# High and low parts of the stationary operands stored in turn, at four distances modulo 256 bytes

## The chip, the cores and the metric

The kernel runs on one core of a Trainium2 chip. The metric is the device time of one execution in microseconds, and the median of the runs is compared. TensorE's granted clock was 0.999 over the profiled execution.

## The reference

A two-layer encoder trunk over 256 tokens of width 2048, all in float32. Layer 0 mixes tokens with a bidirectional mLSTM, layer 1 with a bidirectional HGRN2; each is followed by a gated MLP of inner width 5504 with a depthwise convolution of width 3:

```python
for layer in range(DEPTH):
    hn = rmsnorm(h, norm_mix_g[layer])
    if layer % N_MIXERS == 0:
        mix = mlstm_mixer(hn, mlstm_w_in[j], mlstm_b_gate[j], mlstm_head_g[j], mlstm_w_out[j])
    else:
        mix = hgrn_mixer(hn, hgrn_w_in[j], lower_bounds[layer], hgrn_head_g[j], hgrn_w_out[j])
    h = h + mix
    h = h + conv_glu(rmsnorm(h, norm_ffn_g[layer]), ffn_w_up[layer], ...)
return rmsnorm(h, final_g)
```

Nearly all of the arithmetic is in the projections: `hn @ w_in`, `y @ w_out`, `hn @ w_up` (2048 to 2 x 5504) and `... @ w_down`. The weights, some 440 MB, are read once.

## The kernel before

Every projection is done in split precision. A float32 value is written as a high part (rounded to the format `float32r`) and a low part (the rest, in the same format), and the product is made of three terms: high with high, high with low, low with high.

The work is a list of chunks (class `Chunk`). Chunks of kind "fm" give 256 output features with the tokens along the columns: the weights are the stationary operand of the matmul and the activations the moving one. For each of 16 k-blocks and each of two feature blocks there is a pair of matmuls: line 201, high weights with the 512 columns of `x` (256 tokens high, 256 tokens low), and line 208, low weights with the 256 high columns. The up projections (86 chunks in all), mLSTM's q and k and HGRN's q and gates (`w_bq`) are of this kind. Chunks of kind "tm" give 512 output features with the tokens along the partitions: the activations are stationary and the weights move. For each k-block and each half of the tokens there are three matmuls of 512 columns, lines 191 to 193. v, o and the gates of the mixers are of this kind with the normalised tiles `xt0` to `xt15` as stationary operand; the output projections and the down projections (function `project`) use the tiles `ya`, `yb` and `g`, kept under the tags `yt0` to `yt21` by `slot` (the first 16 in the pool `keep`, the others in the pool `ff`, whose first tile `lead` only moves the following ones). The last seven k-blocks of the last chunk run one token half after the other (lines 178 to 180).

The generator `split_weights` fetches 1 MB of weights at a time on SP's queue into `raw` (three buffers) and cuts it into pieces of 1024 columns. For each piece ScalarE writes the high part `wh` (line 146) and VectorE the low part `wl` as the difference (line 147). There are four buffers of each, and `stream` keeps `LOOK = 3` pieces made ahead. A piece lasts for four k-blocks of an "fm" chunk or two of a "tm" chunk. The first chunk cuts smaller pieces of 640 columns. The activations are split the same way by `split` (lines 213 and 214) and, in the MLP, at lines 832 and 833.

The other work (heads of the mixers, norms, convolution) is pushed as generators on a list `side` and advanced by a planned time (`side.tick`) between the matmuls. In HGRN's `head`, each of seven levels h = 1, 2, 4 ... 64 multiplies alternating blocks of h elements by a gate (lines 698 and 699, through the views `blocks` and `gview`, lines 630 to 636): at h = 1 single elements from two places in turn, at h = 2 two neighbours together.

In memory `wh`, `wl`, `x` and `yt` lie each as contiguous runs: 1024 columns of `wh` in one tile, 1024 of `wl` in another; in `x` and `yt` 256 high columns and then 256 low ones. The stationary operand of one matmul is 128 neighbouring floats. The sizes of the tiles are such that `xt`, `yt` (all 22), `wh` and `wl` all begin at the same place modulo 256 bytes.

Of the kernel before, what the change touches and what calls it, by code (L numbers as in the profile page):

```python
# [8 lines left out]
F32 = mybir.dt.float32  # L9
F32R = mybir.dt.float32r  # L10
I32 = mybir.dt.int32
AF = mybir.ActivationFunctionType
ALU = mybir.AluOpType
PSUM = bass.MemoryType.PSUM

P = 128
T = 256
D = 2048
KT = D // P
# [24 lines left out]
WB = 4  # L44
MIX = 5
LEAD = 48
FIRST = (0, 1, 2, 4, 7, 10, 13, 16)

HALF = 64
# [5 lines left out]
def trunk_kernel(ctx, tc, xT, x_d, fg_d, pp_d, cst_d, w_first, w_aq, w_ak, w_av, w_ao, w_aout,  # L55
                 w_bq, w_bv, w_bg, w_bout, w_up, w_down, out, mscr):
    nc = tc.nc
    act, dve, pool, pe = nc.scalar, nc.vector, nc.gpsimd, nc.tensor

    keep = ctx.enter_context(tc.tile_pool(name="keep", bufs=1))  # L60
    wpool = ctx.enter_context(tc.tile_pool(name="wpool", bufs=1))
# [8 lines left out]
    hmx = keep.tile([P, 2], F32, name="mhalf")  # L70
    hx = keep.tile([P, KT, T], F32, name="hx")
    hT = [hx[:, k] for k in range(KT)]
    hm = hx.rearrange("p k t -> p (k t)").rearrange("p (a c) -> p a c", a=2)
    ident = cst[:, C_ID:C_ID + P]

    def col(name, i):
        o = OFF[name] + i
        return pp[:, o:o + 1]

    def aux(name):  # L80
        return psa.tile([P, 512], F32, tag="aux", name=name)
# [2 lines left out]
    class Side:  # L84
        def __init__(self):
            self.now, self.jobs = 0.0, []
# [26 lines left out]


    class Chunk:
        def __init__(self, kind, src, nk, x, done, before=None, last=False, turns=0):
            self.last, self.turns = last, turns
            self.kind, self.src, self.nk, self.x, self.done, self.before = kind, src, nk, x, done, before
            self.width = {"fm": 256, "tm": 512, "first": 512 + P}[kind]

    def split_weights(chunks):

        first = True
        for ch in chunks:
            total = ch.nk * ch.width
            cuts = [0]
            if first:
                cuts = [k * ch.width for k in FIRST]
            while cuts[-1] < total:
                cuts.append(min(total, cuts[-1] + 2048))  # L130
            step = ch.width if first else 1024
            for b0, b1 in zip(cuts, cuts[1:]):
                n = b1 - b0
                raw = wpool.tile([P, 2048], F32, tag="raw", bufs=RAW, name="raw")
                nc.sync.dma_start(raw[:, :n], ch.src[:, b0:b0 + n])
                if first:
                    k0, k1 = b0 // ch.width, b1 // ch.width
                    (nc.scalar if k0 < 2 else nc.sync).dma_start(hx[:, k0:k1], xT[:, k0:k1])
                    if k0 == 0:
                        nc.scalar.dma_start(pp[:, 0:KT], pp_d[:, 0:KT])  # L140
                for c0 in range(0, n, step):
                    m = min(step, n - c0)
                    wh = wpool.tile([P, 1024], F32R, tag="wh", bufs=WB, name="wh")
                    wl = wpool.tile([P, 1024], F32R, tag="wl", bufs=WB, name="wl")
                    r = raw[:, c0:c0 + m]
                    act.copy(wh[:, :m], r)  # L146
                    dve.tensor_tensor(wl[:, :m], r, wh[:, :m].bitcast(F32), ALU.subtract)  # L147
                    yield wh, wl, m // ch.width
            first = False

    def stream(chunks):
        pieces = split_weights(chunks)
        ready = []

        def fetch():
            p = next(pieces, None)
            if p is not None:
                ready.append(p)

        for _ in range(LOOK):  # L160
            fetch()
        for ch in chunks:
            if ch.before:
                ch.before()
            ps = [psm.tile([P, 512], F32, tag="mm", name="mm") for _ in range(3 if ch.kind == "first" else 2)]
            k = 0
            while k < ch.nk:
                fetch()
                wh, wl, n = ready.pop(0)
                if ch.last and k + sum(p[2] for p in ready) + n == ch.nk:  # L170
                    pieces_, k0 = [(wh, wl, n)] + ready, k
                    for t in range(2):
                        k = k0
                        for wh, wl, n in pieces_:
                            for kk in range(n):
                                x, c = ch.x(k), slice(kk * 512, (kk + 1) * 512)
                                xh, xl = x[:, t * P:(t + 1) * P], x[:, T + t * P:T + (t + 1) * P]
                                pe.matmul(ps[t], xh, wh[:, c], start=False, stop=False)
                                pe.matmul(ps[t], xh, wl[:, c], start=False, stop=False)
                                pe.matmul(ps[t], xl, wh[:, c], start=False, stop=k == ch.nk - 1)  # L180
                                k += 1
                        ch.half(ps[t], t)
                    return
                for kk in range(n):
                    x = ch.x(k)
                    st, sp = k == 0, k == ch.nk - 1
                    if ch.kind != "fm":
                        c = slice(kk * 512, (kk + 1) * 512)
                        for t in range(2):
                            xh, xl = x[:, t * P:(t + 1) * P], x[:, T + t * P:T + (t + 1) * P]  # L190
                            pe.matmul(ps[t], xh, wh[:, c], start=st, stop=False)  # L191
                            pe.matmul(ps[t], xh, wl[:, c], start=False, stop=False)  # L192
                            pe.matmul(ps[t], xl, wh[:, c], start=False, stop=sp)  # L193
                        if ch.kind == "first":
                            pe.matmul(ps[2], wh[:, 512:512 + P], x, start=st, stop=False)
                            pe.matmul(ps[2][:, 0:T], wl[:, 512:512 + P], x[:, 0:T], start=False, stop=sp)
                        side.tick(1.3)
                    else:
                        for f in range(len(ps)):
                            c = kk * ch.width + f * P  # L200
                            pe.matmul(ps[f], wh[:, c:c + P], x, start=st, stop=False)  # L201
                            if f and k == 0 and ch.turns:
                                it = aux("turns")
                                for i in range(ch.turns):
                                    pe.transpose(it[:, i * P:(i + 1) * P], ident, ident)
                            if f:
                                side.tick(0.325 * len(ps))
                            pe.matmul(ps[f][:, 0:T], wl[:, c:c + P], x[:, 0:T], start=False, stop=sp)  # L208
                    k += 1
            ch.done(ps)  # L210

    def split(dst, src, gcol):
        act.activation(dst[:, 0:T], src, AF.Copy, scale=gcol)  # L213
        dve.scalar_tensor_tensor(dst[:, T:2 * T], src, gcol, dst[:, 0:T].bitcast(F32), ALU.mult, ALU.subtract)

    def fm_sum(ps, dst):
        b = ev.tile([P, T], F32, tag="b", bufs=3, name="b")
# [14 lines left out]
    class Norm:  # L232
# [3 lines left out]
            self.xs, self.done = [None] * KT, False  # L236

        def take(self, k, src):
            self.xs[k] = keep.tile([P, 2 * T], F32R, tag=f"xt{k}", name=f"xt{k}")
            split(self.xs[k], src, col(self.g, self.o + k))  # L240

        def squares(self, i, mp):

# [127 lines left out]
    def project(wsrc, nk, x, norm):  # L371

        def done(c):
            def f_(ps):
                for t in range(2):
                    h = hm[:, t, 512 * c:512 * c + 512]
                    dve.tensor_tensor(h, h, ps[t], ALU.add)
                if norm is not None:
                    norm.add(c)
            return f_  # L380
        chunks = [Chunk("tm", wsrc(c), nk, x, done(c)) for c in range(4)]
        if isinstance(norm, FinalNorm):
            chunks[3].last, chunks[3].half = True, norm.half
        return chunks
# [6 lines left out]
    def mlstm(norm, nxt):  # L391
        YT = [None] * KT
# [130 lines left out]
        def finish(st):  # L523
            for j in range(2):
# [3 lines left out]
                pz = aux("pz")  # L528
# [7 lines left out]
                for v in range(2):  # L536
                    i = 2 * (2 * st["pr"] + j) + v
                    YT[i] = slot(i, "ya")
                    split(YT[i], pz[:, v * T:(v + 1) * T], col("a_head_g", i))
                yield  # L540

        chunks = []
# [62 lines left out]
    def hgrn(norm, nxt):  # L605
        YT = [None] * KT
# [139 lines left out]
        def finish(qd, four):  # L746
            for j in range(4):
# [11 lines left out]
                    c = slice(t * P, (t + 1) * P)  # L759
                    pe.transpose(pz[:, c], y[:, c], ident)  # L760
                YT[hd] = slot(hd, "yb")
                split(YT[hd], pz[:, 0:T], col("b_head_g", hd))

        heads = [dict() for _ in range(BH)]
        chunks = []
# [40 lines left out]
    def ffn(layer, norm, nxt):  # L806
# [10 lines left out]
        def done_up(f, i, GT):  # L817
            def go(ps):
# [10 lines left out]
                act.activation(c, c, AF.Gelu)  # L829
                dve.tensor_tensor(c, c, v, ALU.mult)  # L830
                g = slot(i, "g", mp)
                act.copy(g[:, 0:T], c)
                dve.tensor_tensor(g[:, T:2 * T], c, g[:, 0:T].bitcast(F32), ALU.subtract)
                GT.append(g)
            return go

# [117 lines left out]
```

## Time and profile before

| | |
|---|---|
| median of the runs | 2444.94 us (2444.8 to 2445.08) |
| the profiled execution | 2444.99 us, its span 2443.2 us |
| TensorE matmuls | 2431.0 us busy (99%), 13551 instructions |
| VectorE, ScalarE, GpSimd | 1695.7 (69%), 1207.7 (49%), 149.3 us (6%) |
| read from HBM | 447.46 MB, 184 GB/s over the span |

The rows of groups give line, engine, operation, written tile and read tiles, shape and count, then busy time in us, the mean of one in ns, and the idle time just before them with what ended it. PE is TensorE's matmul side, PEld its load of the stationary operand, which runs beside it, DVE VectorE, ACT ScalarE, POOL GpSimd. A matmul's record is longer than the spacing between two of them, because they are pipelined; spacings are read from start to start, or as a stretch of time divided by the number of matmuls in it. In a table of windows each engine's busy time stands with its count of instructions in brackets, and behind them the granted clock, the transfers' share and GB/s.

### The profile page before, as it was taken

The numbers are of one execution on the slowest core, as the hardware profiler recorded it, in microseconds if no ns is written. First come the engines' busy times: TensorE is split into PE (matmuls) and PEld (weight loads), VectorE is DVE, ScalarE is ACT, GpSimd is POOL, SyncE is SP. The second block draws the span as 40 slices with busy tenths as digits, with TensorE's granted clock in tenths as the row PEclk, the third lists the DMA queues.
The fourth block names the chain that finished last, engine by engine and source line by source line (L and its number), as shares of the span: only waits on it lengthen the run. The fifth ranks groups of instructions, "written<-read, shape, count | busy, mean of one in ns | idle before, by whom it ended". The sixth has DMA issues, their size and how long they took to land.

```text
span 2443.2 us, 34691 instructions
## 1 busy us (share of the span) xinstructions
PE 2431.0 (99%) x13551; PEld 2077.7 (85%) x13551; DVE 1695.7 (69%) x2784; ACT 1207.7 (49%) x1831; POOL 149.3 (6%) x219
## 2 busy tenths in 40 slices
PE   9999999999999999999999999999999999999998
PEld 7888888888888888888888888888888888888887
DVE  7766556777645777657888888885777754677754
ACT  6655455444434444445555555545544443444443
POOL 0100000000000000001222222220000000000000
PEclk9999999999999999999999999999999999999999
DMA  7654555555555555555444454445555555555554
GB/s 287 199 180 160 185 179 183 190 190 190 198 190 192 191 190 188 187 181 193 165 163 169 160 173 163 165 165 199 188 190 190 190 189 195 187 187 190 190 184 144
DMA packets 66197, 451.87 MB, mean 185 GB/s; under 512 B 7648, under 2 KB 8160, under 8 KB 13424
## 3 DMA queue, kind: packets, MB, share of 16 engines
q1 hardware_dynamic: 63792, 443.02, 53.0%
q0 software_dynamic: 1232, 5.31, 0.9%
q8 instruction: 106, 1.74, 0.3%
q10 hardware_dynamic: 1008, 1.32, 0.2%
q14 instruction: 59, 0.48, 0.1%
HBM read 447.46 MB, written 2.16 MB: 184 GB/s over the span
## 4 chain that ended last, share of the span: by engine, by line
PE 99%; ACT 0%; DMA 0%; issue 0%; DVE 0%; SPq 0%; POOLq 0%; POOL 0%
PE mm L201 36%; PE mm L208 18%; PE mm L191 13%; PE mm L193 13%; PE mm L192 13%; PE pd L685 1%; PE pn L507 1%; PE py L739 1%; PE pz L275 0%; PE S L493 0%; PE pd L726 0%; DMA raw<-in_w_first 0%; ACT xt L213 0%; PE pd L727 0%; PE pz L760 0%
## 5 line engine op out<-in xcount | busy, mean ns | idle before, releaser
L147 DVE TENSOR_TENSOR wl<-raw,wh 128x1024 fp32r<-128x1024 f32 (+1 forms) x848 | 1031.2, 1218 | 595.2 <-ACT wh L146 586.7
L201 PE MATMUL mm<-xt,wh 128*128 128x512 f32 x3776 | 1321.6, 395 | 0.0
L146 ACT CAST wh<-raw 128x1024 fp32r<-128x1024 f32 (+1 forms) x848 | 881.7, 1041 | 850.2 <-PE mm L193 387.9
L208 PE MATMUL mm<-xt,wl 128*128 128x256 f32 x3776 | 1057.7, 280 | 0.0
L201 PEld LDWEIGHTS mm<-xt,wh 128*128 128x128 f32 x3776 | 709.0, 188 | 161.7
L208 PEld LDWEIGHTS mm<-xt,wl 128*128 128x128 f32 x3776 | 713.3, 189 | 1.7
L193 PE MATMUL mm<-wh,g 128*128 128x512 f32 x674 | 263.1, 390 | 0.0
L191 PE MATMUL mm<-wh,g 128*128 128x512 f32 x674 | 262.8, 390 | 0.0
L192 PE MATMUL mm<-wl,g 128*128 128x512 f32 x674 | 262.6, 390 | 0.0
L191 PE MATMUL mm<-wh,xt 128*128 128x512 f32 x512 | 202.2, 398 | 2.2 <-ACT xt L213 2.2
L192 PE MATMUL mm<-wl,xt 128*128 128x512 f32 x512 | 202.1, 395 | 0.3 <-DVE wl L147 0.3
L193 PE MATMUL mm<-wh,xt 128*128 128x512 f32 x512 | 201.6, 395 | 0.0
L218 ACT COPY b<-mm 128x256 f32<-128x256 f32 x237 | 87.6, 369 | 175.3 <-PE mm L208 175.3
L193 PEld LDWEIGHTS mm<-wh,g 128*128 128x128 f32 x674 | 126.6, 188 | 26.3
L192 PEld LDWEIGHTS mm<-wl,g 128*128 128x128 f32 x674 | 126.7, 188 | 26.1
L191 PEld LDWEIGHTS mm<-wh,g 128*128 128x128 f32 x674 | 126.7, 188 | 25.9
L191 PEld LDWEIGHTS mm<-wh,xt 128*128 128x128 f32 x512 | 96.0, 189 | 22.1 <-ACT xt L213 2.5
L193 PEld LDWEIGHTS mm<-wh,xt 128*128 128x128 f32 x512 | 96.9, 189 | 19.8
L192 PEld LDWEIGHTS mm<-wl,xt 128*128 128x128 f32 x512 | 96.9, 189 | 19.5 <-DVE wl L147 0.8
L219 DVE TENSOR_TENSOR a<-mm,b 128x256 f32<-128x256 f32 x86 | 36.5, 425 | 53.6 <-ACT b L218 53.6
L704 POOL TENSOR_TENSOR G<-G 128x384 f32<-128x384 f32 (+2 forms) x96 | 65.0, 677 | 6.3
L698 DVE TENSOR_TENSOR QK<-QK,G 128x256 f32<-128x256 f32 x112 | 61.5, 549 | 0.3 <-DVE qm L677 0.3
(205 smaller groups left out, 1854.8 us busy)
## 6 DMA issues: line engine op xcount, KB each, us to landing
raw<-in_w_up SPq DMA_DIRECT2D x172, 1024.0 KB, 5.1
raw<-in_w_down SPq DMA_DIRECT2D x80, 1024.0 KB, 4.8
raw<-in_w_bq SPq DMA_DIRECT2D x48, 1024.0 KB, 5.1
raw<-in_w_ao SPq DMA_DIRECT2D x16, 1024.0 KB, 4.9
raw<-in_w_aout SPq DMA_DIRECT2D x16, 1024.0 KB, 4.8
raw<-in_w_bv SPq DMA_DIRECT2D x16, 1024.0 KB, 4.8
raw<-in_w_bg SPq DMA_DIRECT2D x16, 1024.0 KB, 4.8
raw<-in_w_bout SPq DMA_DIRECT2D x16, 1024.0 KB, 4.9
```

What stands on the lines that cost most here:

```text
L146: act.copy(wh[:, :m], r)
L147: dve.tensor_tensor(wl[:, :m], r, wh[:, :m].bitcast(F32), ALU.subtract)
L191: pe.matmul(ps[t], xh, wh[:, c], start=st, stop=False)
L192: pe.matmul(ps[t], xh, wl[:, c], start=False, stop=False)
L193: pe.matmul(ps[t], xl, wh[:, c], start=False, stop=sp)
L201: pe.matmul(ps[f], wh[:, c:c + P], x, start=st, stop=False)
L208: pe.matmul(ps[f][:, 0:T], wl[:, c:c + P], x[:, 0:T], start=False, stop=sp)
L218: act.copy(b, ps[:, T:2 * T])
L219: dve.tensor_tensor(dst, ps[:, 0:T], b, ALU.add)
L507: pe.matmul(pn[:, 0:258], w, v, start=(i == 0), stop=(i == len(parts) - 1))
L698: dve.tensor_tensor(ka, ka, gview(G, n, 1, h), ALU.mult)
L704: pool.tensor_tensor(G2, G[:, 0:6 * n:2], G[:, 1:6 * n:2], ALU.mult)
```

## The change

A piece of weights is now one tile `w` of 2048 + 64 floats in place of the two tiles `wh` and `wl`. For "fm" chunks, high and low parts of one weight are neighbours: `wh` is every second float from 0 and `wl` every second float from 1, and the piece begins 0, 64, 128 or 192 bytes into the tile, by its place in the chunk. For "tm" chunks they stay two contiguous runs. The tiles `yt` are written with high and low parts in turn too, and `project`'s matmuls read them so; `xt` keeps its two runs. All `xt` and `yt` tiles are set up at the start, with a gap of 64 bytes ahead of `yt4`, `yt8`, `yt12` and behind `yt15`. Number, order and operands of the instructions are otherwise those of before.

```diff
+GAP = 16
...
+    for k in range(KT):
+        keep.tile([P, 2 * T], F32R, tag=f"xt{k}", name=f"xt{k}")
+    for k in range(KT):
+        if k % 4 == 0 and k:
+            keep.tile([P, GAP], F32, name=f"gap{k}")
+        keep.tile([P, 2 * T], F32R, tag=f"yt{k}", name=f"yt{k}")
+    keep.tile([P, GAP], F32, name="gap")
...
+    def mixed(t, n):
+
+        return t[:, 0:2 * n:2], t[:, 1:2 * n:2]
...
-                    wh = wpool.tile([P, 1024], F32R, tag="wh", bufs=WB, name="wh")
-                    wl = wpool.tile([P, 1024], F32R, tag="wl", bufs=WB, name="wl")
+                    w = wpool.tile([P, 2048 + 4 * GAP], F32R, tag="w", bufs=WB, name="w")
+                    if ch.kind == "fm":
+                        wh, wl = mixed(w[:, GAP * ((b0 + c0) // 1024 % 4):], m)
+                    else:
+                        wh, wl = w[:, 0:m], w[:, 1024:1024 + m]
                     r = raw[:, c0:c0 + m]
-                    act.copy(wh[:, :m], r)
-                    dve.tensor_tensor(wl[:, :m], r, wh[:, :m].bitcast(F32), ALU.subtract)
+                    act.copy(wh, r)
+                    dve.tensor_tensor(wl, r, wh.bitcast(F32), ALU.subtract)
...
+    def stationary(ch, x, t):
+        ts = slice(t * P, (t + 1) * P)
+        if ch.mixed:
+            return [v[:, ts] for v in mixed(x, T)]
+        return x[:, ts], x[:, T:2 * T][:, ts]
...
-                            xh, xl = x[:, t * P:(t + 1) * P], x[:, T + t * P:T + (t + 1) * P]
+                            xh, xl = stationary(ch, x, t)
...
-        chunks = [Chunk("tm", wsrc(c), nk, x, done(c)) for c in range(4)]
+        chunks = [Chunk("tm", wsrc(c), nk, x, done(c), mixed=True) for c in range(4)]
...
-                    split(YT[i], pz[:, v * T:(v + 1) * T], col("a_head_g", i))
+                    split(*mixed(YT[i], T), pz[:, v * T:(v + 1) * T], col("a_head_g", i))
...
-                act.copy(g[:, 0:T], c)
-                dve.tensor_tensor(g[:, T:2 * T], c, g[:, 0:T].bitcast(F32), ALU.subtract)
+                gh, gl = mixed(g, T)
+                act.copy(gh, c)
+                dve.tensor_tensor(gl, c, gh.bitcast(F32), ALU.subtract)
```

More of the change, by code (lines that the diff above doesn't have):

```diff
@@ L115, in trunk_kernel, with __init__ @@
     class Chunk:
-        def __init__(self, kind, src, nk, x, done, before=None, last=False, turns=0):
-            self.last, self.turns = last, turns
+        def __init__(self, kind, src, nk, x, done, before=None, last=False, turns=0, mixed=False):
+            self.last, self.turns, self.mixed = last, turns, mixed
             self.kind, self.src, self.nk, self.x, self.done, self.before = kind, src, nk, x, done, before
@@ L175, in stream @@
                             for kk in range(n):
-                                x, c = ch.x(k), slice(kk * 512, (kk + 1) * 512)
-                                xh, xl = x[:, t * P:(t + 1) * P], x[:, T + t * P:T + (t + 1) * P]
+                                c = slice(kk * 512, (kk + 1) * 512)
+                                xh, xl = stationary(ch, ch.x(k), t)
                                 pe.matmul(ps[t], xh, wh[:, c], start=False, stop=False)
@@ L189, in stream @@
                         for t in range(2):
-                            xh, xl = x[:, t * P:(t + 1) * P], x[:, T + t * P:T + (t + 1) * P]
+                            xh, xl = stationary(ch, x, t)
                             pe.matmul(ps[t], xh, wh[:, c], start=st, stop=False)
@@ L210, in stream, with split @@
             ch.done(ps)
-    def split(dst, src, gcol):
-        act.activation(dst[:, 0:T], src, AF.Copy, scale=gcol)
-        dve.scalar_tensor_tensor(dst[:, T:2 * T], src, gcol, dst[:, 0:T].bitcast(F32), ALU.mult, ALU.subtract)
+    def split(hi, lo, src, gcol):
+        act.activation(hi, src, AF.Copy, scale=gcol)
+        dve.scalar_tensor_tensor(lo, src, gcol, hi.bitcast(F32), ALU.mult, ALU.subtract)
     def fm_sum(ps, dst):
@@ L238, in take @@
         def take(self, k, src):
-            self.xs[k] = keep.tile([P, 2 * T], F32R, tag=f"xt{k}", name=f"xt{k}")
-            split(self.xs[k], src, col(self.g, self.o + k))
+            x = self.xs[k] = keep.tile([P, 2 * T], F32R, tag=f"xt{k}", name=f"xt{k}")
+            split(x[:, 0:T], x[:, T:2 * T], src, col(self.g, self.o + k))
         def squares(self, i, mp):
@@ L761, in finish @@
                 YT[hd] = slot(hd, "yb")
-                split(YT[hd], pz[:, 0:T], col("b_head_g", hd))
+                split(*mixed(YT[hd], T), pz[:, 0:T], col("b_head_g", hd))
         heads = [dict() for _ in range(BH)]
```

## The prediction

> **What bounds the kernel now.** I read the page from the top: busy shares, then the chain that ended last, then the costliest groups.
>
> ```profile
> span 2443.2 us, 34691 instructions
> PE 2431.0 (99%) x13551; PEld 2077.7 (85%) x13551; DVE 1695.7 (69%) x2784; ACT 1207.7 (49%) x1831; POOL 149.3 (6%) x219
> ...
> PE 99%; ACT 0%; DMA 0%; issue 0%; DVE 0%; SPq 0%; POOLq 0%; POOL 0%
> PE mm L201 36%; PE mm L208 18%; PE mm L191 13%; PE mm L193 13%; PE mm L192 13%; PE pd L685 1%; PE pn L507 1%; PE py L739 1%; PE pz L275 0%; PE S L493 0%; PE pd L726 0%; DMA raw<-in_w_first 0%; ACT xt L213 0%; PE pd L727 0%; PE pz L760 0%
> ...
> L147 DVE TENSOR_TENSOR wl<-raw,wh 128x1024 fp32r<-128x1024 f32 (+1 forms) x848 | 1031.2, 1218 | 595.2 <-ACT wh L146 586.7
> L201 PE MATMUL mm<-xt,wh 128*128 128x512 f32 x3776 | 1321.6, 395 | 0.0
> L146 ACT CAST wh<-raw 128x1024 fp32r<-128x1024 f32 (+1 forms) x848 | 881.7, 1041 | 850.2 <-PE mm L193 387.9
> L208 PE MATMUL mm<-xt,wl 128*128 128x256 f32 x3776 | 1057.7, 280 | 0.0
> ```
>
> The whole chain is TensorE, with idle 0.0 ahead of the two largest groups. Nothing else is late: ACT's cast spends its idle time waiting for PE to free a buffer. So the time is the number of matmuls times their spacing, and only a change of the spacing counts. The 395 ns of one matmul is a pipelined record; its spacing comes from the stages. Windows of an up projection, a down projection and the HGRN layer, then the first and the third alone for line 201:
>
> ```profile
> core 0: us, PE busy (x) PEld busy (x) DVE busy (x) ACT busy (x) POOL busy (x), PEclk, DMA share, GB/s
> 420.00:620.00 200.00, 200.00 (x1155) 175.08 (x1154) 146.74 (x236) 100.54 (x147) 0.00 (x0) 1.00 0.57 192
> 650.00:740.00 90.00, 90.00 (x399) 74.61 (x398) 45.04 (x44) 35.75 (x36) 0.00 (x0) 1.00 0.57 193
> 1120.00:1280.00 160.00, 160.00 (x1079) 137.33 (x1078) 135.50 (x277) 84.13 (x149) 39.35 (x55) 1.00 0.50 170
> ...
> 420.00:620.00 200.00, 200.00 (x578) 108.55 (x577) 1.00 0.57 192
> 1120.00:1280.00 160.00, 98.09 (x278) 51.91 (x277) 1.00 0.50 170
> ```
>
> In the up projection a pair (lines 201 and 208, 512 and 256 columns, each with a fresh stationary operand) takes 200 / 578 = 0.346 us. In a down projection a matmul of 512 columns takes 90 / 399 = 0.226. The timeline there, first and last of fourteen (13 spacings), with one weight load:
>
> ```profile
> 699.93 0.39 PE L191 MATMUL mm<-wh,g 128*128 128x512 f32 x1
> ...
> 700.16 0.19 PEld L193 LDWEIGHTS mm<-wh,g 128*128 128x128 f32 x1
> ...
> 702.88 0.39 PE L192 MATMUL mm<-wl,g 128*128 128x512 f32 x1
> ```
>
> 2.95 / 13 = 0.227 us, used below. The load for the next matmul starts with the matmul before it and takes 0.19, so both reads of SBUF run at once: the stationary operand's 512 bytes per partition and the moving operand's 2048.
>
> **Is there anything to win in the spacing?** The plain float32 matmuls of lines 493 and 739 are the comparison. One source call makes two records (16 calls at line 493, 32 records), each with a load of its own.
>
> ```profile
> L493 PE MATMUL S<-q,k x32: 377/378/381, 66.9 to 290.2; 128*128 128x256 f32 x32
> 66.87 1.03 PE L493 MATMUL S<-q,k 128*128 128x256 f32 x4
> L739 PE MATMUL py<-V,AT x128: 270/275/276, 1180.4 to 1642.0; 128*128 128x128 f32 x128
> 1197.39 1.05 PE L739 MATMUL py<-V,AT 128*128 128x128 f32 x8
> ```
>
> Line 493: (1.03 - 0.378) / 3 = 0.217 us for 256 columns. Line 739: (1.05 - 0.275) / 7 = 0.111 for 128 columns and one load. From 128 to 256 columns that is 0.83 ns a column. If a column of the high/low matmuls takes half of that, 512 take the array time of line 493, yet the spacing is 0.227 and not 0.217. In the up projection the pair takes 0.346 against 0.217 + 0.111 = 0.328. So 0.010 us of each down matmul and 0.018 of each up pair are not array time. My reading, a theory: moving reads and load get in each other's way. In lines 493 and 739 both walk at one pace (4 bytes per 0.83 ns, a load of 128 columns fitting in 0.111). In the others the moving read walks twice as fast as the load, so that it passes it again and again. With the stationary operand at every second element, the load walks 8 bytes a column and keeps the moving read's pace.
>
> **The change part by part.** No instruction, transfer or queue entry is added, removed or moved past another; only addresses change.
>
> (a) Stationary reads. Touched: all 3776 pairs of lines 201 and 208, and the projections' matmuls with g, ya or yb:
>
> ```profile
> L191 PE MATMUL mm<-wh,g 128*128 128x512 f32 x674 | 262.8, 390 | 0.0
> L191 PE MATMUL mm<-wh,xt 128*128 128x512 f32 x512 | 202.2, 398 | 2.2 <-ACT xt L213 2.2
> L191 PE MATMUL mm<-wh,yb 128*128 128x512 f32 x128 | 50.7, 396 | 0.0
> L191 PE MATMUL mm<-wh,ya 128*128 128x512 f32 x128 | 50.4, 394 | 0.0
> L178 PE MATMUL mm<-wh,g 128*128 128x512 f32 x14 | 5.3, 390 | 0.0
> ```
>
> (674 + 128 + 128 + 14) x 3 = 2832 matmuls; those with xt (512 x 3) keep their layout. Bounds: at best the spacing falls to the plain rows', 3776 x 0.018 + 2832 x 0.010 = 68 + 28 = 96 us. At worst the doubled stretch doubles the interference, the same 96 us lost, or the load slows (below). I take the gain, for the plain rows at equal pace are the nearest, but for three of the four distances only: in step, the distance decides whether the reads meet, and one of four steps of 64 bytes may be bad. 0.75 x 96 = 72 us.
>
> (b) The load's own time. No row has a stationary operand with gaps. Lower bound: no cost. Upper bound: its time grows with the bytes walked, 2 x 0.111 = 0.222. In a down matmul that still lies under 0.227; in an up pair two loads make 0.444 against 0.346, +0.098 x 3776 = +370 us. I take nothing, by the nearest row, VectorE's:
>
> ```profile
> 1337.90 0.62 DVE L699 TENSOR_TENSOR QK<-QK,G 128x256 f32<-128x256 f32 x1
> ...
> 1340.25 0.41 DVE L699 TENSOR_TENSOR QK<-QK,G 128x256 f32<-128x256 f32 x1
> ```
>
> The first is level h = 1, where each element lies far from the one before (views `blocks` and `gview`). The second is h = 2, where two neighbours come together, and costs no more than later levels. Every second float is nearer to the second. [...]
>
> (c) Writing with gaps, lines 146, 147, 213, 214, 832, 833. VectorE between 0 and (0.62 - 0.41) / 256 x 1024 = 0.84 us a piece; ScalarE between 0 and a doubling, 1.04. I take 0, by h = 2. What hides it: VectorE is at 146.74 of 200 in the up projection and 135.50 of 160 in the HGRN layer, ScalarE at half. The doubling would leave ScalarE at 100.5 + 72 x 1.04 = 175 of 200, still hidden, since pieces are made three ahead (8 pairs each, 3 x 8 x 0.346 = 8.3 us). With VectorE's upper bound the cover is gone: a rival below.
>
> (d) One tile for both halves. If a matmul of the high part should now also wait for VectorE's low part, the three pieces of lead cover its 1.22 us. Behind that matmul all of PE would be queued. Only the first chunk has no lead: 16 pieces of at most 0.82 us (the row of line 147 at 640 elements), 13 us at most, below nothing excluded since no wait goes; I take 0, as start-up is paced by the transfers.
>
> ```profile
> L147 DVE TENSOR_TENSOR wl<-raw,wh 128x640 fp32r<-128x640 f32 x16 | 12.7, 823 | 8.7 <-ACT wh L146 8.7
> ```
>
> (e) Gaps and tiles set up ahead: addresses only. The four gaps of 64 bytes make 256, so tiles behind them stay where they were modulo 256.
>
> Sum: the profiled run took 2444.99 us (1.8 outside its span), against a median of 2444.94; 2445 - 72 = **2373**. What is late next: with the fast stages 3 to 4% shorter VectorE comes to 76% in up and 88% in HGRN, and the transfers' share from 0.57 to 0.59; neither ends the chain.
>
> **The rivals.**
>
> - **No change, 2445.** The 10 ns may belong to exchanging operands in this number format, not to SBUF reads. For it: the spacing is the same for wh with g as with xt, ya and yb (390 to 398 ns a record). Against it: lines 493 and 739 exchange operands as often. [...]
> - **A toll on the stretch read (slower).** If the load costs the moving read something for each 16, 32 or 64 bytes it walks over, 1024 bytes cost twice what 512 do: +96, 2541. For it: the excess is there with every load. Against it: an up pair with two loads has 0.018, not clearly 2 x 0.010, and the plain rows pay no such toll.
> - **In step and colliding (slower).** At one pace two reads that meet meet all the way. A quarter of the 3776 x 2 + 2832 = 10384 loads is 2596; each may cost up to a load's 0.111, +288 - 72 = 2661. It decides from 72 / 2596 = 0.028 us a meeting load; the middle, 0.055, gives 2517. Against it: one short stall would part the two reads.
> - **VectorE becomes the bound.** With 0.84 more a piece, the up window's 578 / 8 = 72 pieces make 146.7 + 61 = 208 of 200, and the HGRN window's 278 / 8 = 35 make 135.5 + 29 = 165 of 160: 4% of 952 us (86 chunks of 32 x 0.346) and 3% of some 470 (the row below), +52, less the 21 won in the projections: 2476. Against it: level h = 2 of (b).
>
> ```profile
> L685 PE MATMUL pd<-q,ks x128: 221/222/223, 1153.4 to 1621.9; 128*64 128x64 f32 x128
> ```
>
> - **The load slows** as in (b): 2815.
>
> **How the numbers follow.** Forecast 0.45, no change 0.15, toll 0.17, collision 0.12, VectorE 0.07, slow load 0.04. A measurement of this kernel tells about 2% from no change. Faster by over 2%: 0.45. Within: no change and half of VectorE's case, 0.19. Slower: 0.36. The forecast's own range is 2335 (all four distances good is 2349, and 14 us more, since the plain rows' 0.217 is read from times rounded to 10 ns) to 2395 (half of the gain). The range that holds 8 in 10 has to reach the toll and the middle collision: 2335 to 2580. It leaves out the slow load and the hard collision.
>
> **What would show it.** Right: the down spacing of lines 191 to 193 falls from 0.227 towards 0.217 with g, ya and yb but not with xt; the up pair from 0.346 towards 0.328; with one k in four groups of four perhaps worse; lines 146 and 147 keep 1.04 and 1.22 us; PE stays at 99% of the chain. Wrong: a down spacing at 0.237 and a pair at 0.364 (toll); a quarter of the pairs far longer than the rest (collision); loads above 0.19; waits of PE for wl at line 147 (VectorE); or nothing moved at all.

## The result and the profile after

The changed kernel takes 2478.24 us (2477.32 to 2479.15) against 2444.94 us: ratio 1.0136, 95% interval 1.0093 to 1.018. It is 33 us slower; 2373 us was forecast, in a range from 2335 to 2580 us, with the faster case as the likeliest.

The page of the changed kernel: busy shares, the chain, and the groups that answer to those of before. One tile `w` stands for `wh` and `wl`, so the lines have moved: 201 is now 222, 208 is 229, 191 to 193 are 212 to 214, 146 and 147 are 161 and 162.

```profile
span 2475.5 us, 34430 instructions
PE 2462.3 (99%) x13551; PEld 2131.9 (86%) x13551; DVE 1699.4 (69%) x2784; ACT 1259.7 (51%) x1831; POOL 148.4 (6%) x219
...
PE 99%; ACT 0%; DMA 0%; issue 0%; DVE 0%; SPq 0%; POOLq 0%; POOL 0%
...
L162 DVE TENSOR_TENSOR w<-raw,w 128x1024 fp32r<-128x1024 f32 (+1 forms) x848 | 1035.0, 1221 | 639.1 <-ACT w L161 632.4
L161 ACT CAST w<-raw 128x1024 fp32r<-128x1024 f32 (+1 forms) x848 | 921.8, 1088 | 889.0 <-PE mm L214 413.8
L222 PE MATMUL mm<-xt,w 128*128 128x512 f32 x3776 | 1339.0, 398 | 0.0
L229 PE MATMUL mm<-xt,w 128*128 128x256 f32 x3776 | 1062.1, 281 | 0.0
L222 PEld LDWEIGHTS mm<-xt,w 128*128 128x128 f32 x3776 | 738.3, 196 | 142.2
L214 PEld LDWEIGHTS mm<-w,g 128*128 128x128 f32 x674 | 130.8, 194 | 25.8
L212 PEld LDWEIGHTS mm<-w,xt 128*128 128x128 f32 x512 | 95.6, 188 | 23.6 <-ACT xt L234 3.1
```

The same two rows of loads before, whose stationary operand was contiguous:

```profile
L201 PEld LDWEIGHTS mm<-xt,wh 128*128 128x128 f32 x3776 | 709.0, 188 | 161.7
L193 PEld LDWEIGHTS mm<-wh,g 128*128 128x128 f32 x674 | 126.6, 188 | 26.3
```

TensorE is still the whole chain, with no idle time ahead of its large groups. VectorE's pieces take 3 ns more in the mean (1218 to 1221), ScalarE's 47 ns (1041 to 1088), both hidden. These means count the contiguous pieces too: in the window below, where all pieces have gaps, ScalarE's go from 75.53 / 72 = 1.05 us to 80.31 / 71 = 1.13. What moved is TensorE's own records: the loads with gaps take 194 to 196 ns where contiguous ones take 188, and those of `xt`, which stayed contiguous, still take 188. The instructions fell from 34691 to 34430 with the counts of every engine's work unchanged: what went are waits on semaphores (VectorE's from 902 to 645, ScalarE's from 839 to 827, and 8 more on GpSimd and TensorE), since a piece is one tile now.

The window of the up projection, whole and for line 222 alone (columns as before):

```profile
core 0: us, PE busy (x) PEld busy (x) DVE busy (x) ACT busy (x) POOL busy (x), PEclk, DMA share, GB/s
420.00:620.00 200.00, 200.00 (x1135) 178.41 (x1134) 145.21 (x229) 105.59 (x143) 0.00 (x0) 1.00 0.54 188
...
420.00:620.00 200.00, 200.00 (x568) 110.79 (x567) 1.00 0.54 188
```

A pair takes 200 / 568 = 0.352 us instead of 0.346. That gap isn't the same in all up chunks. Before, the last 21 up chunks of layer 1 already took 200 / 567 = 0.353 (1134 matmuls, two to a pair), with the same layout as the others, and they take 0.353 now:

```profile
2090.00:2290.00 200.00, 200.00 (x1134) 173.49 (x1133) 143.39 (x231) 96.70 (x141) 0.00 (x0) 1.00 0.55 185
```

In the timeline of the first down chunk, these are the first matmuls of k-blocks 0, 4, 8, 12 and 16 (24 spacings from each to the next) and the last one of line 212 (33 spacings behind):

```profile
653.86 0.39 PE L212 MATMUL mm<-w,g 128*128 128x512 f32 x1
659.45 0.39 PE L212 MATMUL mm<-w,g 128*128 128x512 f32 x1
664.97 0.40 PE L212 MATMUL mm<-w,g 128*128 128x512 f32 x1
670.53 0.39 PE L212 MATMUL mm<-w,g 128*128 128x512 f32 x1
676.13 0.39 PE L212 MATMUL mm<-w,g 128*128 128x512 f32 x1
683.83 0.39 PE L212 MATMUL mm<-w,g 128*128 128x512 f32 x1
```

That is 0.233 us a matmul at distance 0, 0.230 at 64 bytes, 0.232 at 128, 0.233 at 192, and 0.233 in the tiles behind, which are at distance 0 again; before it was 0.227 throughout. All four distances lose, and the best loses 3 ns.

The sum of all spacings (from each matmul's start to the next one's), by stationary operand, in us:

| | before | after | difference |
|---|---|---|---|
| up-type pairs (weights stationary) | 1328.6 | 1347.8 | +19.2 |
| projections with g, ya, yb | 645.4 | 660.7 | +15.3 |
| v, o, gates with xt | 360.5 | 357.5 | -3.0 |
| all others | 98.6 | 99.5 | +0.9 |

The four differences make 32.4, and the span grew by 32.3. The first row holds the 32 matmuls of the first chunk's 128 extra columns too, which wait at the start and make 1.6 of the 19.2; the 3776 pairs alone went from 1322.3 to 1339.9. The median spacing with xt is 227 ns in both kernels; what that row lost is waiting. So the loss is in the matmuls whose stationary operand got gaps or a new place.

### The profile page after: what moved, and what is told of

The parts are those of the page before. It is cut to its first block, busy times and chain, and to the rows that moved or that the text cites. A ratio compares the mean times of both kernels' runs of the same rounds, so it can differ in the third digit from the quotient of the medians.

```text
span 2475.5 us, 34430 instructions
## 1 busy us (share of the span) xinstructions
PE 2462.3 (99%) x13551; PEld 2131.9 (86%) x13551; DVE 1699.4 (69%) x2784; ACT 1259.7 (51%) x1831; POOL 148.4 (6%) x219
## 4 chain that ended last, share of the span: by engine, by line
PE 99%; ACT 0%; DMA 0%; issue 0%; DVE 0%; SPq 0%; POOLq 0%; POOL 0%
PE mm L222 36%; PE mm L229 18%; PE mm L212 13%; PE mm L213 13%; PE mm L214 13%; PE pd L706 1%; PE pn L528 1%; PE py L760 1%; PE pz L296 0%; PE S L514 0%; PE pd L747 0%; DMA raw<-in_w_first 0%; ACT xt L234 0%; PE pd L748 0%; PE pz L781 0%
## 5 line engine op out<-in xcount | busy, mean ns | idle before, releaser
L162 DVE TENSOR_TENSOR w<-raw,w 128x1024 fp32r<-128x1024 f32 (+1 forms) x848 | 1035.0, 1221 | 639.1 <-ACT w L161 632.4
L161 ACT CAST w<-raw 128x1024 fp32r<-128x1024 f32 (+1 forms) x848 | 921.8, 1088 | 889.0 <-PE mm L214 413.8
L222 PE MATMUL mm<-xt,w 128*128 128x512 f32 x3776 | 1339.0, 398 | 0.0
L229 PE MATMUL mm<-xt,w 128*128 128x256 f32 x3776 | 1062.1, 281 | 0.0
L222 PEld LDWEIGHTS mm<-xt,w 128*128 128x128 f32 x3776 | 738.3, 196 | 142.2
L229 PEld LDWEIGHTS mm<-xt,w 128*128 128x128 f32 x3776 | 741.9, 196 | 1.3
L214 PE MATMUL mm<-w,g 128*128 128x512 f32 x674 | 265.9, 395 | 0.0
L212 PE MATMUL mm<-w,g 128*128 128x512 f32 x674 | 265.7, 394 | 0.0
L213 PE MATMUL mm<-w,g 128*128 128x512 f32 x674 | 265.3, 394 | 0.0
L212 PE MATMUL mm<-w,xt 128*128 128x512 f32 x512 | 200.7, 395 | 3.1 <-ACT xt L234 2.4
L213 PE MATMUL mm<-w,xt 128*128 128x512 f32 x512 | 201.7, 394 | 0.4 <-DVE w L162 0.4
L214 PE MATMUL mm<-w,xt 128*128 128x512 f32 x512 | 199.9, 392 | 0.0
L214 PEld LDWEIGHTS mm<-w,g 128*128 128x128 f32 x674 | 130.8, 194 | 25.8
L212 PEld LDWEIGHTS mm<-w,g 128*128 128x128 f32 x674 | 130.8, 194 | 25.8
L213 PEld LDWEIGHTS mm<-w,g 128*128 128x128 f32 x674 | 130.9, 194 | 25.5
L212 PEld LDWEIGHTS mm<-w,xt 128*128 128x128 f32 x512 | 95.6, 188 | 23.6 <-ACT xt L234 3.1
L213 PEld LDWEIGHTS mm<-w,xt 128*128 128x128 f32 x512 | 96.5, 188 | 19.8 <-DVE w L162 0.8
L214 PEld LDWEIGHTS mm<-w,xt 128*128 128x128 f32 x512 | 96.2, 188 | 19.7
```

The lines of the kernel that those rows point to most:

```text
L161: act.copy(wh, r)
L162: dve.tensor_tensor(wl, r, wh.bitcast(F32), ALU.subtract)
```

## The experiments

Theory A is the prediction's frame turned round: the load's reading costs the moving read something, and a load that walks 1024 bytes costs more than one of 512. Rival B: the distances do the harm. Rival C: the writes with gaps disturb TensorE. Rival D (later E): most of the spacing above the columns' time is a fixed price that has nothing to do with what is read.

**In turn, at one distance.**

```diff
-                        wh, wl = mixed(w[:, GAP * ((b0 + c0) // 1024 % 4):], m)
+                        wh, wl = mixed(w, m)
# and no gap tiles among the y tiles
```

> High and low parts in turn as in the changed kernel, but no gaps: every piece of weights and every y tile at distance 0 modulo 256 bytes from the moving operand. Theory A (the load with gaps costs the moving read more at every distance; the four distances only vary the amount): by the spacings of the changed kernel at its distance 0 (pair 0.353 us against 0.3495 before, projections 0.233 against 0.227), +13 and +17 us: 2475 us. Rival B (the distances do the harm, storing in turn is free): 2445 us. Rival C (the writes with gaps by ScalarE and VectorE disturb TensorE's reads): 2478 us, as the writes are the same.

Measured: 2480.35 us against 2445.02, ratio 1.0143 (1.0128 to 1.0158). B falls as the whole cause: without the distances the loss is all there. Between A (2475 expected) and C (2478) the time doesn't decide.

**Distances alone.**

```diff
-        return t[:, 0:2 * n:2], t[:, 1:2 * n:2]
+        return t[:, 0:n], t[:, n:2 * n]
# pieces: wh = w[:, o:o + m], wl = w[:, 1024 + o:1024 + o + m] with o = GAP * (piece % 4)
```

> The four distances alone: pieces of weights begin 0, 64, 128 or 192 bytes into their tile and the y tiles keep their gaps, but high and low parts stay contiguous runs. Theory A: the faster moving read passes a contiguous load at any distance, so 2445 us within 3. Rival B (the distances do the harm): 2478 us. Rival C: 2445 us.

Measured: 2456.91 us, ratio 1.0047 (1.003 to 1.0063), +12 us: neither 2445 nor 2478. The sums of spacings give the place: up-type pairs +3.8, projections +8.7. A contiguous y tile away from distance 0 costs the projections as well. Theory A, in which the place of a contiguous load doesn't matter, was wrong in that.

**Weights in turn, y tiles contiguous.**

```diff
-        chunks = [Chunk("tm", wsrc(c), nk, x, done(c), mixed=True) for c in range(4)]
+        chunks = [Chunk("tm", wsrc(c), nk, x, done(c)) for c in range(4)]
# and g, ya, yb written as two runs; the gaps stay
```

> Pieces of weights in turn at four distances as in the changed kernel, the y tiles as contiguous runs (with their gaps). All theories: the projections' matmuls go back to 0.227 us, 2832 x 0.006 = 16 us of the 33 return: 2462 us. If the two parts do not add up (2470 or more, or 2450 or less), something other than the spacing by stationary operand is at work.

Measured: 2470.78 us, ratio 1.0103 (1.0088 to 1.0118). Only 7.5 us came back, not 16: the sum of the projections is 654.1, just that of the run before, since the gaps alone cost them 8.7. The pairs' sum is 1347.5, that of the changed kernel. So the weights in turn cost 19 us, the y tiles' gaps 9, and the y tiles in turn on top of their gaps 6.6. The expectation called 2470 us a sign of something else at work: it was the price of the gap tiles, which it had put at nothing.

**What is read, with the writes as before.** The heart of the matter: the layout is that of before, and only the addresses of the stationary operand change from chunk to chunk (line 223 every float, 226 every second, 229 every fourth, 232 one float 128 times; in the projections 198 and 203 for every float and every second).

```diff
+                                elif q == 2:
+                                    pe.matmul(ps[f], wh[:, o:o + 2 * P:2], x, start=st, stop=False)
...
+                                elif q == 4:
+                                    pe.matmul(ps[f], wh[:, o:o + 4 * P:4], x, start=st, stop=False)
...
+                                    pe.matmul(ps[f], wh[:, o:o + 1].broadcast_to([P, P]), x, start=st, stop=False)
```

> The kernel before, with everything written and laid out as there; only what TensorE reads as its stationary operand is changed, by chunk (so the output is not the reference's): in the 43 up chunks of each layer every first, second or fourth float, or one float 128 times, begun at 16 places 16 bytes apart (4 places for the last two); in the down projections every first or second float at 8 places. Theory A: up pairs 0.346 to 0.349 us at every first float whatever the place, 0.351 to 0.357 at every second, more again at every fourth (2048 bytes walked; 0.360 or more), and towards 0.328 with one float. Rival C (it is the writes): 0.346 to 0.349 for all. Rival D (a fixed price of exchanging the stationary operand): the same for all, one float too.

The groups of loads, then from the timeline the first and 64th matmul of 512 columns with one float (63 pairs), the first and the 65th with every fourth (64 pairs), the first and 42nd of line 203 with every second (123 spacings), and the first matmuls of the four projection chunks with every float at 0, 64, 128 and 192 bytes (132 spacings from each to the next) with the last matmul of the fourth (131 spacings behind):

```profile
L223 PEld LDWEIGHTS mm<-xt,wh 128*128 128x128 f32 x1216 | 228.3, 188 | 53.4
L226 PEld LDWEIGHTS mm<-xt,wh 128*128 128x128 f32 x1024 | 200.1, 195 | 39.2
L229 PEld LDWEIGHTS mm<-xt,wh 128*128 128x128 f32 x256 | 79.9, 312 | 0.1
L232 PEld LDWEIGHTS mm<-xt,wh 128*128 128x128 f32 x256 | 48.6, 190 | 10.5
...
944.14 0.40 PE L232 MATMUL mm<-xt,wh 128*128 128x512 f32 x1
965.98 0.39 PE L232 MATMUL mm<-xt,wh 128*128 128x512 f32 x1
...
883.79 0.52 PE L229 MATMUL mm<-xt,wh 128*128 128x512 f32 x1
913.97 0.51 PE L229 MATMUL mm<-xt,wh 128*128 128x512 f32 x1
...
1022.43 0.40 PE L203 MATMUL mm<-wh,g 128*128 128x512 f32 x1
1051.14 0.39 PE L203 MATMUL mm<-wh,g 128*128 128x512 f32 x1
...
649.07 0.40 PE L198 MATMUL mm<-wh,g 128*128 128x512 f32 x1
679.03 0.40 PE L198 MATMUL mm<-wh,g 128*128 128x512 f32 x1
709.83 0.39 PE L198 MATMUL mm<-wh,g 128*128 128x512 f32 x1
740.51 0.40 PE L198 MATMUL mm<-wh,g 128*128 128x512 f32 x1
770.50 0.40 PE L200 MATMUL mm<-wh,g 128*128 128x512 f32 x1
```

- One float: 21.84 / 63 = 0.347 us a pair, as much as a contiguous operand (0.346 in the window of before). A load that walks nothing saves nothing. That ends theory A: most of the excess over 0.328 is not the load's reading. D stands.
- Every second float, distance 0, in a projection: 28.71 / 123 = 0.233, the changed kernel's spacing to the nanosecond, with contiguous writes. At 64, 128 and 192 bytes the table has 0.230, 0.231 and 0.233, again the changed kernel's. C is out: the writes are not the cause, what TensorE reads is.
- Every float in the projections: 29.96 / 132 = 0.227 at distance 0, 30.80 / 132 = 0.233 at 64 bytes, 30.68 / 132 = 0.232 at 128 and 29.99 / 131 = 0.229 at 192. A contiguous run is the better one at 0 and at 192 bytes, but at 64 bytes every second float takes 3 ns less, and at 128 bytes 1 ns less. So gaps are not worse everywhere. The layout of before had its y tiles at the one of these distances where a contiguous run takes 0.227, and either the gaps or the distances alone are enough to lose that.
- Every fourth float, each in 16 bytes of its own: the load's record goes from 188 to 312 ns and the pair to 30.18 / 64 = 0.472. The load side sits idle 0.1 us ahead of these loads, against 10.5 for as many loads of one float: here the load itself has become the bound.
- The pairs with every float lie at 0.347 to 0.354 by place, those with every second at 0.349 to 0.360. Place by place, every second float takes 3 to 7 ns more at eight of the 16 places, the same within 1 ns at seven and 2 ns less at one (64 bytes); over the 16 the means are 0.3505 and 0.3529.

**Is it a fixed price?** A second table: the weights of each up chunk placed 0 to 63 floats into their tile, and in the projections g read as one float, with fewer columns, and with fewer moving columns.

```diff
+                    wh = wpool.tile([P, 1088], F32R, tag="wh", bufs=WB, name="wh")[:, o:o + 1024]
...
+                                    xh, xl = [v[:, 0:1].broadcast_to([P, P]) for v in (xh, xl)]
...
+                                    pe.matmul(ps[t][:m], a_, b_[:, c], start=False, stop=sp and p_ == 2)
...
+                                    pe.matmul(ps[t][:, 0:n], a_, b_[:, c], start=False, stop=sp and p_ == 2)
```

> The kernel before with two tables. (1) Up chunks: the contiguous weights are written and read 0 to 63 floats further into their tile, another number for each of the 43 chunks of a layer; nothing is left out there. If the distance sets a small part of the spacing, the pair is 0.3465 to 0.348 us at 4, 8, 12 and 56 floats, 0.350 to 0.355 at 0, 16 and 60, as in the table of reads; if the reads' places in that table were special, no such order. (2) Down projections (most k-blocks, so the output is not the reference's): stationary g read at 0 to 60 floats, one float 128 times, with 64 or 32 columns, or with 384, 256 or 128 moving columns. Theory E (a fixed price of 12 ns a matmul, whatever is read): 0.227 with one float, with 64 and with 32 columns; 0.174 us at 384 moving columns and 0.120 at 256 (0.217 scaled, plus 0.010). Rival A (the load's reads cost it): towards 0.217 with one float, 64 and 32 columns. Rival F (the high/low format takes longer for each column): 0.170 at 384, 0.1135 at 256, and no change with one float or fewer columns.

First and last matmul of a chunk in its timeline: contiguous (120 matmuls), one float (120), 384 and 256 moving columns (120 each), 64 and 32 stationary columns (114 each); then the loads of 128, 64 and 32 columns:

```profile
650.49 0.39 PE L204 MATMUL mm<-wh,g 128*128 128x512 f32 x1
677.46 0.39 PE L204 MATMUL mm<-wh,g 128*128 128x512 f32 x1
...
1975.85 0.40 PE L206 MATMUL mm<-wh,g 128*128 128x512 f32 x1
2003.36 0.39 PE L206 MATMUL mm<-wh,g 128*128 128x512 f32 x1
...
2006.30 0.33 PE L210 MATMUL mm<-wh,g 128*128 128x384 f32 x1
2026.95 0.33 PE L210 MATMUL mm<-wh,g 128*128 128x384 f32 x1
...
2029.89 0.28 PE L212 MATMUL mm<-wh,g 128*128 128x256 f32 x1
2044.16 0.28 PE L212 MATMUL mm<-wh,g 128*128 128x256 f32 x1
...
2299.83 0.39 PE L208 MATMUL mm<-wh,g 128*64 128x512 f32 x1
2325.81 0.40 PE L208 MATMUL mm<-wh,g 128*64 128x512 f32 x1
...
2328.78 0.39 PE L208 MATMUL mm<-wh,g 128*32 128x512 f32 x1
2354.96 0.40 PE L208 MATMUL mm<-wh,g 128*32 128x512 f32 x1
...
L204 PEld LDWEIGHTS mm<-wh,g 128*128 128x128 f32 x700 | 131.1, 188 | 29.7
L208 PEld LDWEIGHTS mm<-wh,g 128*64 128x64 f32 x76 | 10.2, 134 | 7.2
L208 PEld LDWEIGHTS mm<-wh,g 128*32 128x32 f32 x76 | 8.3, 109 | 9.3
```

512 columns 26.97 / 119 = 0.2266, 384 columns 20.65 / 119 = 0.1735, 256 columns 14.27 / 119 = 0.1199. Each 128 columns are worth 53 to 54 ns, 0.417 ns a column, and 13 ns remain at these three widths. That is E, and not a slower column (F: 0.170 and 0.1135). A load of 64 columns (25.98 / 113 = 0.230), of 32 (26.18 / 113 = 0.232) or of one float (27.51 / 119 = 0.231) doesn't lower it, though the load's record falls from 188 to 134 and 109 ns; these come out 3 to 5 ns above the contiguous one, which was expected of none. With 128 moving columns the same law gives 0.067, but the table's matmuls of that width take 0.113 in the window from 2049 to 2059 us (85 in 9.57 us of busy time), about as long as line 739's (0.111) with as many columns and a load each. Something else bounds there, which wasn't followed up. A pair at the fixed price alone is 0.2266 + 0.1199 = 0.3465. In the table of pairs the places fall as expected at 4, 12 and 56 floats (0.3465 to 0.347) and at 16 and 60 (0.353), but 8 floats have 0.353 and distance 0 has 0.347, the other way round than in the first table. Before a whole kernel was tried at 1 float, that place was read as 0.3425, under all others; it has 0.350 (next part). (The whole times of the tables mix all cases and are not compared.)

**Can a better place win?** The tables seemed to name places of contiguous weights at or under that floor. Each was put into the whole kernel: 32 bytes (0.3467 a pair in the first table), 4 bytes (read as 0.3425 in the second), and 196 bytes for high with 4 for low parts (0.3467 in a third).

```diff
+                    o = SHIFT if ch.kind == "fm" else 0
+                    wh = wpool.tile([P, 1088], F32R, tag="wh", bufs=WB, name="wh")[:, o:o + 1024]
+                    wl = wpool.tile([P, 1088], F32R, tag="wl", bufs=WB, name="wl")[:, o:o + 1024]
```

> The kernel before, with the contiguous weights of the up-type chunks begun 8 floats (32 bytes) into their tile, y tiles and everything else at distance 0. If the distance is what is left to win: pair 0.3467 against 0.3495 us, 3776 x 0.0028 = 10.6 us less: 2434 us. If the place of the contiguous run does not matter, 2445 us.

> The kernel before, the contiguous weights of the up-type chunks begun one float (4 bytes) into their tile. The second table had 0.3425 us a pair in the one chunk of each layer laid out so, under the 0.347 of the best others. If that holds over the kernel: 3776 x (0.3495 - 0.3425) = 26 us less, 2419 us. If a spacing read from one chunk does not carry over (as at 32 bytes, where 10.6 us less were expected and 1.6 more came): 2445 us within 3.

> The kernel before with a third table: up chunks with separate places of high and low weights (one float and others), four chunks of a layer with both at one float, two at 0; down projections with stationary g read at 1 to 8 and 48 to 63 floats (so the output is not the reference's). If one float is a good place by itself, all eight chunks with it show 0.3425; if it was the neighbourhood of the chunk in time, they differ by 4 ns or more. In the projections, if 0.227 is the floor of a fixed price, none of the 15 places is under 0.2265; if a place can undercut it as one float did for the pairs (224 ns behind the 512 columns), some show 0.224.

> The kernel before, the contiguous weights of the up-type chunks begun 49 floats (high) and 1 float (low) into their tiles: the place in the third table whose two chunks showed 226.7 ns behind the 512 columns and 120.0 behind the 256, just the fixed price's 226.7 and 119.9 with no interference. If places carry over from a chunk to the kernel: 3776 x (0.3493 - 0.3467) = 10 us less, 2435 us. If they do not (32 bytes and 4 bytes did not): 2445 to 2455 us.

Measured: 32 bytes 2446.58 us, ratio 1.0007 (0.9998 to 1.0016); 4 bytes 2450.28, 1.0023 (1.0014 to 1.0033); 196 and 4 bytes 2445.90, 1.0003 (0.9994 to 1.0012). None wins: the first and the last can't be told from before, and 4 bytes cost 5 us. Two readings behind the expectations fail.

The first is the 0.3425. These are the first matmuls of two pairs of the chunk at 1 float in the second table, 29 pairs apart:

```profile
414.33 0.39 PE L226 MATMUL mm<-xt,wh 128*128 128x512 f32 x1
424.48 0.39 PE L226 MATMUL mm<-xt,wh 128*128 128x512 f32 x1
```

10.15 / 29 = 0.350, and no gain. Near the start of this chunk two matmuls of 512 columns follow each other, so that the two widths no longer take turns. Whoever counts every second spacing of the chunk as one behind 512 columns mixes the widths and gets the 224 ns that the expectation of the third table names. Four of the third table's six chunks with both parts at 4 bytes have 0.350 as well (the other two are interrupted by other work), its four at distance 0 have 0.3466 to 0.347, and the whole kernel at 4 bytes has 0.350 in all its up chunks but the first of each layer. So this place did carry over from the table. No up chunk of any run lies below 0.3465: the fixed price was never undercut.

The second is the 0.3495 against which places were compared. It is the mean of all pairs of the kernel before. Of its 86 up chunks 63 are at 0.3465 to 0.347 already; the mean is raised by the mixers' pairs (0.347 to 0.356) and by the last 21 up chunks (0.353). At 32 bytes these 21 stay at 0.353. At 196 and 4 bytes, the second half of layer 0's up chunks has 0.3467 and the others 0.3495. So the spacing that a place settles into depends on more than the place modulo 256 bytes; on what, stays open. In the projections, none of 15 places undercut 0.2267; 3 and 57 floats equalled it, as 4 and 60 did in the second table, and the others were at 0.229 to 0.234.

**In turn, at the best single distances.**

```diff
-                        wh, wl = mixed(w[:, GAP * ((b0 + c0) // 1024 % 4):], m)
+                        wh, wl = mixed(w[:, 36:], m)
# all y tiles 64 bytes from the weights' place
```

> High and low parts in turn as in the changed kernel, but at the best single distances seen: weights 144 bytes (0.349 us a pair in the first table), all y tiles 64 bytes (0.2305 in the changed kernel). If the loss is the distances' and a good one repairs it: 2445 us or less. If storing in turn costs at every distance (theory E: it adds to the interference, never takes from the fixed price): pair 0.349 to 0.353, projections 0.2305, 0 to 13 and 2832 x 0.0035 = 10 us: 2453 to 2468 us.

Measured: 2455.60 us, ratio 1.0045 (1.003 to 1.0061), with the projections at 0.230 throughout. That takes 23 of the 33 us back and is still slower than before: no distance tried makes storing in turn pay. What is left is nearly all in the projections (sum 654.5 against 645.4); the 3776 pairs with weights in turn at 144 bytes make 1323.7 us against 1322.3, so there the gaps cost almost nothing.

## Why the prediction was wrong

- **What bounds the kernel** held: TensorE's spacing decides, and the sum of spacings grew by what the span grew.
- **The step that failed is the comparison with lines 493 and 739**, where the prediction took 0.217 us as what 512 high/low columns would take without interference. Half of the plain rows' 0.83 ns a column was right (0.417 measured); wrong was the assumption that nothing beyond the plain rows' remainder (0.217 - 256 x 0.83, 4 to 5 ns) would stay. 13 ns a matmul or more remain with one float, with 32 columns and at 384 and 256 columns. Against that price a projection at 0.227 has no interference to lose, and a pair at 0.346 next to none. The 96 us to be won did not exist; all pairs of before lie 1322.3 - 3776 x 0.3465 = 14 us above that price.
- **Part (a)'s sign** failed with it. The new addresses added 3 to 6 ns to each projection matmul and 5 to a pair in the mean (17.6 us / 3776): +15.3 and +19.2 in the table in place of -21 and -51. The theory of equal paces, on which three good distances of four rested, has no support: none of four was good in the projections, nor, against 0.346, in the up pairs (0.351 to 0.356).
- **The toll rival** (+96, 2541) had the direction but not the law: twice the stretch cost 3 to 6 ns of 227, not another 10, and one float gave nothing back. **The no-change rival** came nearest and missed only the small loss on top: no layout tried took a projection's matmul below 0.227 us or the pairs of an up chunk below 0.3465, though whether the exchange or the format sets that price was not shown. The one-float pairs agree with it (0.347 against 0.346); it doesn't cover the 229 to 233 ns against 226.7 that the load's addresses alone make in the projections.
- **Collision** did not show: no quarter of the matmuls was far longer than the rest. That 2478 us lies in the stated range, and within 3 us of the VectorE rival's 2476, is luck: the range reached that far for collisions and a toll of 10 ns, and TensorE was never without work for VectorE's sake in the large groups.
- **Parts (b) and (c)** came out nearly as costed: loads 6 to 8 ns longer instead of none or twice as long, VectorE 3 ns a piece, ScalarE under a tenth. The row of level h = 2 was the right neighbour. That VectorE's rows stand for TensorE's load was the author's estimate; with every fourth float, one to 16 bytes, a load took 312 ns.
- **Parts (d) and (e)** held, except that the gaps among the y tiles alone cost 8.7 us when the tiles are contiguous, an edit that was costed at nothing. The start hardly moved: line 213's first matmul in the chain begins at 17.97 us, that of line 192 before at 17.89. The transfers pace only a part of that, 1.65 to 7.78 us in the chain of before; ScalarE's and VectorE's pieces follow.

## What to carry to other kernels

Before a gap between a measured spacing and another instruction's is counted as something to win, take the suspected cause away on the chip: one stationary operand read as a single float would have shown that the 13 ns stay. Move a stationary operand only with its place in view: in the projections a contiguous run took 0.227 at some places and up to 0.234 at others, and every second float never less than 0.230; in the up pairs every fourth float made the load the bound. Compare a spacing read from one chunk with that same chunk before, as a stretch of time divided by its pairs, and not with the mean of the kernel: three places that looked 10 to 26 us better gained nothing.

## What the runs showed of the hardware

With contiguous loads, a projection's matmul took 226.7 ns at distance 0 and at 3, 4, 57 and 60 floats, and 228.7 to 234.3 at all other places tried. With contiguous loads or every second float, the pairs of an up chunk took 346.5 to 362 ns in the mean, many of them near 346.7, 350.0 and 353.3, and one layout took 346.6 ns in some up chunks of the kernel before and 353.2 in others. So the load's address sets part of the spacing, and in the pairs something in the surroundings does too. What this comes from, and whether the fixed 13 ns belong to the exchange of the stationary operand or to each matmul of this format, stays open: a matmul without a load of its own wasn't tried.
